# The embedding's gate taken early and corrected expert by expert

## The chip, the cores and the metric

The kernel runs on one core of a Trainium2 chip, in one launch. The metric is the device time of the core in microseconds: 706.93 before, the median of three runs (704.91 to 707.18).

## The reference

One layer of a decoder: token mixers (attention and mLSTM), then a mixture of 32 experts of which each token takes two, then an embedding per layer, and a last norm. The change touches the part from the experts on (T = 256 tokens, D = 1024):

```python
h = h + hierarchical_moe(rmsnorm(h, ffn_norm_g[i]), ...)     # per expert: (silu(x@w_gate) * (x@w_up)) @ w_down, weighted
ple_gate = jax.nn.sigmoid(rmsnorm(h, ple_norm_g[i]) @ w_ple_gate[i])   # 1024 x 1024, float32
h = h + (p[i] @ w_ple_proj[i]) * ple_gate
return rmsnorm(h, final_norm_g)
```

## The kernel before

h is held in SBUF as two blocks b of 128 tokens. The experts e = 0 to 31 are taken in eight quads q of four. For a quad, `dispatch` gathers up to 32 tokens per expert with 0/1 matrices og into xe (matmuls px), and builds the weights dwT (transposes pdw). Then `expert` works on one expert's 32 columns of xe:

- pg, gate and up products: 32 matmuls of 256 columns ("gu" in what follows), each of 32 stationary columns, four side by side on the array; the profile counts two records for a float32 matmul, so 64;
- sg = silu on ScalarE, hid = sg * up on VectorE, pht = its transpose on TensorE, hT = its copy;
- pd, the down products: 16 matmuls (32 records);
- four copies of pd into the expert's 32 rows of eo, ScalarE and VectorE in turn.

After a quad, `combine` spreads eo's 128 rows to the tokens with dwT and adds them to h: four products ps of 512 columns, four adds.

An expert's weights are three loads of 2 MB, two of gu and one of down, all issued by SyncE (SP), each into a slot of the ring `slot` (NRING = 10 slots of 16 KB a partition). A slot that is free goes to the next that asks; a tile that is used to the end keeps it. Up to eight of SP's loads are in flight, since each has one of eight DMA semaphores (DMAHW0 to DMAHW7) to itself.

An expert may have more than 32 tokens. `overflow`, after quad LOOP_AT = 3, counts them and loops over what is left, inside `tc.If(n_rv > 0)`. With these inputs the branch is not taken: the profile has no row of the loop. All engines load n_it and branch there, and instructions do not move across it.

`embed` (p @ w_ple_proj, into pe) stands after quad 5 and uses two slots, wpp and ES; ES stays. The gate comes after the last quad: `load_gate` issues its 4 MB behind expert 31's loads, `split_gate` splits them into two float32r parts (ghi, glo), `transpose_h` does the same for h, and `gate_mm` takes three products for each pair, 120 matmuls. `warm` puts 18 matmuls without use among the last expert's. The tail is tanh, times pe, add to h, square and sum, power on GpSimd (POOL), last scaling, and the output.

A scheduler sets each engine's order when the program is built, after the order of the code and its own costs; on the chip each engine takes its instructions in that order.

Of the kernel before, what the change touches and what calls it, by code (L numbers as in the profile page):

```python
# [36 lines left out]
WARM = (7, 4, 3, 1, 3)  # L37
LO_POOL = (11, 101)
NRING = 10
LOOP_AT = 3  # L40

# [6 lines left out]
def layer(ctx: ExitStack, tc: tile.TileContext, A, dbg=None):  # L48
# [661 lines left out]

    def load_gu(t, e, k0, n):
        nc.sync.dma_start(out=t, in_=wgu_v[e][:, k0:k0 + n])
        return [t[:, k] for k in range(n)]

    def load_expert(e):
        def load_dn(t, j, n):
            nc.sync.dma_start(out=t, in_=wd_v[e][:, j:j + n])
# [67 lines left out]
    def expert(wts, xe, i, eo, row, last=False, rest=None):  # L785


        gu, dn = wts
        pe_ins = []

        def pe(ins):
            if last and pe_ins:
                after(ins, pe_ins[-1])
            pe_ins.append(ins)
            return ins

        def warm(n):
            if last:
                pw = psm.tile([P, 512], F32, name="pw", tag="px", bufs=1)
                for _ in range(n):  # L800
                    pe(mm(pw, identb, identb[:, None, :].to_broadcast([P, 4, P]), start=True, stop=True))

        pg = psm.tile([P, 2, P], F32, name="pg", tag="pg", bufs=2)
        for k in range(KD):
            if k == 4:
                warm(WARM[0])
                if rest is not None:
                    rest(4, ins)
            for j in range(4):
                ins = pe(mm(pg[32 * j:32 * j + 32], xe[:, k, 32 * i:32 * i + 32], gu[k][:, :, j * P:(j + 1) * P],  # L810
                      start=(k == 0), stop=(k == KD - 1)))
        warm(WARM[1])
# [5 lines left out]
        pe(nc.tensor.transpose(pt, hid, ident))  # L818
        warm(WARM[2])
# [3 lines left out]
        for j in range(4):  # L823
            if j == 2:
                warm(WARM[3])
            for c in range(4):
                pe(mm(pd[32 * c:32 * c + 32], hT[:, 32 * j:32 * j + 32], dn[j][:, c * 256:(c + 1) * 256],  # L827
                      start=(j == 0), stop=(j == 3)))
        warm(WARM[4])
        for c in range(4):  # L830
            dst = eo[row:row + 32, c * 256:(c + 1) * 256]
# [13 lines left out]
    def overflow():  # L845
# [32 lines left out]
        with tc.If(n_rv > 0):  # L878
            with tc.For_i(0, n_rv, 1):
# [25 lines left out]
    def embed():  # L905
# [20 lines left out]
        return pe, gfin  # L926


    def load_gate():
# [6 lines left out]
        nc.sync.dma_start(out=gfin, in_=A["final_norm_g"].rearrange("(o d) -> o d", o=1).to_broadcast([P, D]))  # L936
        return out

    def split_gate(k):
        if k % 4 == 0:  # L940
            gw.append((slot([P, 4, D], F32R, name="ghi"), slot([P, 4, D], F32R, name="glo")))
        hi, lo = gw[k // 4]
        return split(hi[:, k % 4], lo[:, k % 4], wpl[k // 4][:, k % 4], lo_on=nc.gpsimd if k in (0, 1, 3, 5) else None)

    for q in range(NQ):
        dwT, xe, rest = dispatch(float(q * QUAD * ESTR) if q else None, code, P)
        eo = mo.tile([P, D], F32, name="eo", bufs=1)
        for i in range(QUAD):
            e = q * QUAD + i
            wt = load_expert(e)  # L950
            if e == NE - 1:
                wpl = load_gate()
            expert(wt, xe, i, eo, 32 * i, last=(e == NE - 1), rest=rest if i == 0 else None)
        if q < NQ - 1:
            for c in range(2):
                for b in range(NB):
                    combine(dwT, eo, P, b, c)
        if q == LOOP_AT:
            overflow()
        if q == NQ - 3:  # L960
            pe, gfin = embed()


    gw = []
    HT = slot([P, 2, KD, T], F32R, name="HT")

    def transpose_h(k):
        pt = psm.tile([P, 2, T], F32, name="pt", tag="tp", bufs=2)
        for b in range(NB):
            for kk in range(2):  # L970
                nc.tensor.transpose(pt[:, kk, b * P:(b + 1) * P], h[:, b, (k + kk) * P:(k + kk + 1) * P], ident)
        for kk in range(2):
            ins = split(HT[:, 0, k + kk], HT[:, 1, k + kk], pt[:, kk], scale=col("g3", k + kk), low=True)
        return ins

    split_gate(0)
    combine(dwT, eo, P, 0, 0)
    combine(dwT, eo, P, 1, 0)
    split_gate(1)
    transpose_h(0)  # L980
    combine(dwT, eo, P, 0, 1)
    lo = transpose_h(2)
    after(combine(dwT, eo, P, 1, 1), lo)
    split_gate(2)
    transpose_h(4)
    transpose_h(6)
    for k in range(3, KD):
        last = split_gate(k)
# [7 lines left out]
    rstd_of(r3[:, 0:NB], ss3[:, 0:NB], D, NB)
    nc.vector.tensor_scalar(r3[:, 0:NB], r3[:, 0:NB], 0.5, None, op0=OP.mult)
    out_v = A["out"].rearrange("o (b p) d -> p (o b) d", p=P)

    parts = [(0, 0, 512, "pg"), (0, 512, 512, "pg"), (1, 0, 512, "ps"), (1, 512, 256, "ps"), (1, 768, 256, "px")]  # L1000
    pg = [psm.tile([P, n], F32, name=f"G{b}{c0}", tag=tag, bufs=1 if tag == "px" else 2) for b, c0, n, tag in parts]

    def gate_mm(i, k):
        b, c0, n, _ = parts[i]
        hi, lo = gw[k // 4]
        bs, cs, kk = slice(b * P, (b + 1) * P), slice(c0, c0 + n), k % 4
        mm(pg[i], HT[:, 0, k, bs], hi[:, kk, cs], start=(k == 0), stop=False)
        mm(pg[i], HT[:, 1, k, bs], hi[:, kk, cs], start=False, stop=False)
        mm(pg[i], HT[:, 0, k, bs], lo[:, kk, cs], start=False, stop=(k == KD - 1))

    hn = []
    junk = mo.tile([P, 512], F32, name="junk", tag="xe", bufs=1)
    for k in range(KD // 2):
        for i in range(len(parts)):
            gate_mm(i, k)
    for i, (b, c0, n, _) in enumerate(parts):
        cs = slice(c0, c0 + n)
        for k in range(KD // 2, KD):
            gate_mm(i, k)
        sg = mo.tile([P, 512], F32, name="sg3", tag="ov")  # L1020
        th = nc.scalar.activation(sg[:, 0:n], pg[i], AF.Tanh, scale=r3[:, b:b + 1])
        nc.vector.scalar_tensor_tensor(sg[:, 0:n], sg[:, 0:n], 1.0, pe[:, b, cs], op0=OP.add, op1=OP.mult)
        hn.append(nc.vector.tensor_tensor(h[:, b, cs], h[:, b, cs], sg[:, 0:n], op=OP.add))
        if i in (0, 2, 3):
            nc.gpsimd.tensor_tensor(y[:, b, cs], h[:, b, cs], gfin[:, cs], op=OP.mult)
        for j in {2: (), 3: (), 4: (2, 3, 4)}.get(i, (i,)):
            pb, p0, m, _ = parts[j]
            s_, rb_ = ss3[:, 2 + j:3 + j], r3[:, 2 + pb:3 + pb]
            sq = nc.scalar.activation(junk[:, 0:m], h[:, pb, p0:p0 + m], AF.Square, scale=D ** -0.5, accum_out=s_)
            after(sq, th)  # L1030
            if j in (1, 3):
                nc.vector.scalar_tensor_tensor(s_, s_, EPS, ss3[:, 1 + j:2 + j], op0=OP.add, op1=OP.add)
            elif j == 4:
                nc.vector.tensor_tensor(s_, s_, ss3[:, 1 + j:2 + j], op=OP.add)
            if j in (1, 4):
                nc.gpsimd.tensor_tensor(rb_, s_, mhalf[:, 0:1], op=OP.pow)
    for b in range(NB):
        for i, (pb, c0, n, _) in enumerate(parts):
            if pb != b:
                continue  # L1040
            cs, rb_ = slice(c0, c0 + n), r3[:, 2 + b:3 + b]
            if i == 0:
                nc.gpsimd.tensor_scalar(y[:, b, cs], y[:, b, cs], rb_, None, op0=OP.mult)
            elif i == 2:
                nc.scalar.activation(y[:, b, cs], y[:, b, cs], AF.Copy, scale=rb_)
            elif i == 3:
                nc.vector.tensor_scalar(y[:, b, cs], y[:, b, cs], rb_, None, op0=OP.mult)
            else:
                after(nc.vector.scalar_tensor_tensor(y[:, b, cs], h[:, b, cs], rb_, gfin[:, cs],
                                                     op0=OP.mult, op1=OP.mult), hn[4])  # L1050
# [46 lines left out]
```

## Time and profile before

| | |
|---|---|
| median of three runs | 706.93 us |
| the profiled run, and its span | 706.04 us, 704.3 us |
| PE (TensorE's matmuls) busy | 560.9 us, 80% |
| DVE (VectorE), ACT (ScalarE), POOL busy | 280.7, 186.1, 38.2 us |
| DMA | 241.98 MB, mean 344 GB/s |
| the chain that ended last | 48% DMA, 44% PE |
| mean granted clock of TensorE | 0.916 of full |

Times in rows are from the span's start. An idle time in brackets is the engine's before the row, with what ended it.

### The profile page before, as it was taken

What the parts mean: (1) busy time and instruction counts of PE and PEld (TensorE: products, weight loads), DVE (VectorE), ACT (ScalarE), POOL (GpSimd) and SP (SyncE); (2) the same over time, 40 slices, a digit from 0 to 9 for tenths busy, and PEclk for the clock granted to TensorE, in tenths of its full rate; (3) what the DMA queues carried; (4) which work ended last, traced back from release to release, by engine and by line L of the source; (5) the groups of instructions that cost most, each with busy time, mean ns of one, the idle gap of its engine ahead of it and who ended that gap; (6) DMA issues with size and microseconds to landing.
All of it is one profiled execution on the core that took longest, in us unless ns stands there. A gap on an engine that the chain in (4) does not pass through costs nothing.

```text
span 704.3 us, 12210 instructions
## 1 busy us (share of the span) xinstructions
PE 560.9 (80%) x5161; PEld 382.3 (54%) x5161; DVE 280.7 (40%) x684; ACT 186.1 (26%) x423; POOL 38.2 (5%) x59
## 2 busy tenths in 40 slices
PE   7999999999999998685686564967746956765894
PEld 7898778899986554342334231733423433432384
DVE  4898667676665343141022024312211310311175
ACT  6675556465453211001000000010000210000163
POOL 3000000001300000000000000000000000000063
PEclk9999999999999999899669886898978997988998
DMA  7946533338777899999999997999999999999921
GB/s 268 429 205 248 228 122 120 120 120 333 305 327 299 333 428 428 428 424 429 423 428 426 430 426 316 429 423 430 426 426 424 425 427 427 429 428 424 419 99 60
DMA packets 22130, 241.98 MB, mean 344 GB/s; under 512 B 4708, under 2 KB 5304, under 8 KB 7096
## 3 DMA queue, kind: packets, MB, share of 16 engines
q1 hardware_dynamic: 22056, 241.16, 82.5%
q8 instruction: 42, 0.69, 0.4%
q14 instruction: 16, 0.13, 0.0%
q10 hardware_dynamic: 16, 0.00, 0.0%
HBM read 240.10 MB, written 1.05 MB: 342 GB/s over the span
## 4 chain that ended last, share of the span: by engine, by line
DMA 48%; PE 44%; DVE 4%; ACT 2%; issue 1%; POOL 1%; POOLq 0%; SPq 0%; DVEq 0%; ACTq 0%
DMA wt<-in_expert_gu 31%; DMA wt<-in_expert_down 17%; PE pg L810 5%; PE po L330 4%; PE po L331 4%; PE po L332 4%; PE ps L839 3%; PE po L347 2%; PE po L346 2%; PE po L348 2%; PE pd L827 2%; PE px L761 2%; PE ps L923 1%; PE pyy L470 1%; DMA wt<-in_w_mix 1%
## 5 line engine op out<-in xcount | busy, mean ns | idle before, releaser
L810 PE MATMUL pg<-wt,xe 128*32 128x256 f32 x2032 | 153.6, 438 | 69.8 <-DMA wt<-in_expert_gu 69.8
L810 PEld LDWEIGHTS pg<-wt,xe 128*32 128x32 f32 x2032 | 73.3, 122 | 136.8 <-issue 55.6
L827 PE MATMUL pd<-wt,hT 128*32 128x256 f32 x1024 | 73.6, 434 | 22.8 <-DMA wt<-in_expert_down 18.6
L833 DVE COPY eo<-pd 32x256 f32<-32x256 f32 x64 | 27.1, 423 | 114.5 <-ACT eo L835 114.4
L827 PEld LDWEIGHTS pd<-wt,hT 128*32 128x32 f32 x1024 | 37.9, 121 | 47.4 <-issue 32.9
L835 ACT ACTIVATE eo<-pd 32x256 f32<-32x256 f32 x64 | 23.9, 374 | 150.3 <-PE pd L827 132.0
L816 DVE TENSOR_TENSOR hid<-sg,pg 128x128 f32<-128x128 f32 x32 | 9.2, 288 | 126.0 <-ACT sg L814 126.0
L220 DVE TENSOR_TENSOR wlo<-wt,whi 128x512 fp32r<-128x512 f32 x76 | 51.5, 685 | 18.3 <-ACT whi L219 18.1
L219 ACT ACTIVATE whi<-wt 128x512 fp32r<-128x512 f32 x77 | 47.3, 626 | 32.0 <-PE po L348 16.7
L814 ACT ACTIVATE sg<-pg 128x128 f32<-128x128 f32 x32 | 8.9, 277 | 168.7 <-PE pg L810 168.6
L761 PE MATMUL px<-og,y 128*128 128x128 f32 x256 | 39.6, 308 | 10.3 <-DVE og L752 6.8
L761 PEld LDWEIGHTS px<-og,y 128*128 128x128 f32 x256 | 35.5, 216 | 22.1 <-PEq L878 7.7
L839 PE MATMUL ps<-eo,dwT 128*128 128x512 f32 x64 | 34.2, 661 | 8.8 <-DVE eo L833 8.7
L332 PE MATMUL po<-XT,wlo 128*128 128x256 f32 x144 | 40.4, 280 | 1.0 <-DVE wlo L220 1.0
L330 PE MATMUL po<-XT,whi 128*128 128x256 f32 x144 | 40.6, 282 | 0.0
L331 PE MATMUL po<-XT,whi 128*128 128x256 f32 x144 | 40.3, 280 | 0.0
L765 DVE TENSOR_TENSOR xe<-px,cols 128x256 f32<-128x256 f32 x32 | 13.6, 424 | 61.5 <-PE pg L810 38.9
L220 POOL TENSOR_TENSOR glo<-wt,ghi 128x1024 fp32r<-128x1024 f32 x4 | 10.6, 2671 | 449.4 <-DMA wt<-in_w_ple_gate 448.6
L332 PEld LDWEIGHTS po<-XT,wlo 128*128 128x128 f32 x144 | 27.0, 188 | 1.2 <-DVE wlo L220 1.2
L220 DVE TENSOR_TENSOR spare<-wt,spare 128x512 fp32r<-128x512 f32 x34 | 23.3, 687 | 9.9 <-ACT spare L219 9.8
L331 PEld LDWEIGHTS po<-XT,whi 128*128 128x128 f32 x144 | 27.1, 188 | 0.2 <-issue 0.2
L330 PEld LDWEIGHTS po<-XT,whi 128*128 128x128 f32 x144 | 27.1, 188 | 0.0
(371 smaller groups left out, 956.9 us busy)
## 6 DMA issues: line engine op xcount, KB each, us to landing
wt<-in_expert_gu SPq DMA_DIRECT2D x63, 2048.0 KB, 38.2
wt<-in_expert_down SPq DMA_DIRECT2D x30, 2048.0 KB, 36.5
wt<-in_w_mix SPq DMA_DIRECT2D x10, 2048.0 KB, 22.2
wt<-in_w_up SPq DMA_DIRECT2D x2, 2048.0 KB, 8.5
wt<-in_w_out SPq DMA_DIRECT2D x2, 2048.0 KB
wt<-in_expert_down SPq DMA_DIRECT2D x4, 1024.0 KB
wt<-in_w_ple_gate SPq DMA_DIRECT2D x4, 1024.0 KB, 27.0
wt<-in_w_mix SPq DMA_DIRECT2D x4, 512.0 KB, 7.0
```

The source lines that it names most:

```text
L219: a = nc.scalar.activation(dst_hi, src, AF.Copy)
L220: b = (lo_on or nc.vector).tensor_tensor(dst_lo, src, dst_hi.bitcast(F32), op=OP.subtract)
L330: mm(out[:, f], whi[:, kk], ahi[:, k], start=(k == 0), stop=False)
L331: mm(out[:, f], whi[:, kk], alo[:, k], start=False, stop=False)
L332: mm(out[:, f], wlo[:, kk], ahi[:, k], start=False, stop=(k == kn - 1))
L346: mm(outs[b], ahi[:, k, bs], whi[:, k - k0], start=(k == 0), stop=False)
L761: ins = mm(px[:, k], y[:, b, kc:kc + P], og[:, b], start=(b == 0), stop=(b == NB - 1))
L810: ins = pe(mm(pg[32 * j:32 * j + 32], xe[:, k, 32 * i:32 * i + 32], gu[k][:, :, j * P:(j + 1) * P], start=(k == 0), stop=(k == KD - 1)))
L827: pe(mm(pd[32 * c:32 * c + 32], hT[:, 32 * j:32 * j + 32], dn[j][:, c * 256:(c + 1) * 256], start=(j == 0), stop=(j == 3)))
L833: nc.vector.tensor_copy(out=dst, in_=pd[32 * c:32 * c + 32])
L835: nc.scalar.activation(dst, pd[32 * c:32 * c + 32], AF.Copy)
L839: mm(ps, dwT[0:n, b], eo[0:n, c * 512:(c + 1) * 512], start=True, stop=True)
```

## The change

The gate is no longer taken at the end. When expert 20's loads are issued (GATE_AT = 5), the gate's weights are loaded into two slots that they keep, and `gate_of_h` takes G = (h * g3) @ w_gate for h as it then is, in plain float32. For each later expert `gate_of_rows` transposes its rows of eo, scales them (eT), multiplies by the gate's weights (pq, the shape of a gu) and keeps the rows in eg_rows; these are spread with dwT and added to G as eo is to h. The root mean square, which multiplies the whole row, comes in at the end. In the last quad the first two experts are combined early, and the last expert's rows go through `gate_of_rows` after the loop. The splits and the warming matmuls go. `embed` moves from quad 5 to behind `overflow`, and takes the load of gfin with it. Experts 16 and 17 are loaded ahead of `overflow`, on GpSimd's queue (NPOOL = 2).

```diff
+GATE_AT = 5
+NPOOL = 2
+    def queue(e):
+        return nc.gpsimd if QUAD * (LOOP_AT + 1) <= e < QUAD * (LOOP_AT + 1) + NPOOL else nc.sync
     def load_gu(t, e, k0, n):
-        nc.sync.dma_start(out=t, in_=wgu_v[e][:, k0:k0 + n])
+        queue(e).dma_start(out=t, in_=wgu_v[e][:, k0:k0 + n])
...
+    def spread(dwT, rows_, r0, r1, b, c):
+        ps = psm.tile([P, 512], F32, name="ps", tag="ps", bufs=2)
+        mm(ps, dwT[r0:r1, b], rows_[r0:r1, c * 512:(c + 1) * 512], start=True, stop=True)
+        return ps
+    def combine(dwT, rows_, r0, r1, b, c, into=None):
+        ps = spread(dwT, rows_, r0, r1, b, c)
+        dst = (h if into is None else into)[:, b, c * 512:(c + 1) * 512]
+        return nc.vector.tensor_tensor(dst, ps, dst, op=OP.add)
...
+    def gate_of_h():
+        GH = slot([P, 4096], name="GH")
...
+        for b in range(NB):
+            for c in range(2):
+                ps = psm.tile([P, 512], F32, name="ps", tag="ps", bufs=2)
+                for k in range(KD):
+                    mm(ps, HT[:, k, b * P:(b + 1) * P], wpg[k][:, c * 512:(c + 1) * 512],
+                       start=(k == 0), stop=(k == KD - 1))
+                nc.scalar.activation(G[:, b, c * 512:(c + 1) * 512], ps, AF.Copy)
+    def gate_of_rows(eo, row, eg):
+        pt = psm.tile([P, KD, CAP], F32, name="pet", tag="tp", bufs=2)
+        rs = slice(row, row + CAP)
+        for k in range(KD):
+            nc.tensor.transpose(pt[:, k], eo[rs, k * P:(k + 1) * P], ident[rs, rs])
+        eT = mo.tile([P, KD, CAP], F32, name="eT", tag="le", bufs=1)
+        nc.vector.tensor_tensor(eT, pt, g3k[:, :, None].to_broadcast([P, KD, CAP]), op=OP.mult)
+        pq = psm.tile([P, 256], F32, name="pq", tag="px", bufs=1)
+        for k in range(KD):
+            for c in range(4):
+                mm(pq[32 * c:32 * c + 32], eT[:, k], wpg[k][:, c * 256:(c + 1) * 256],
+                   start=(k == 0), stop=(k == KD - 1))
+        as_rows(eg, row, pq)
     for q in range(NQ):
...
-            wt = load_expert(e)
-            if e == NE - 1:
-                wpl = load_gate()
-            expert(wt, xe, i, eo, 32 * i, last=(e == NE - 1), rest=rest if i == 0 else None)
+            wt = ahead.pop(e, None) or load_expert(e)
+            if e == QUAD * GATE_AT:
+                wpg = load_gate()
+                G = gate_of_h()
+            expert(wt, xe, i, eo, 32 * i, rest=rest if i == 0 else None)
+            if q >= GATE_AT and e < NE - 1:
+                gate_of_rows(eo, 32 * i, eg_rows)
+            if q == NQ - 1 and i == 1:
+                for into, rows_ in ((None, eo), (G, eg_rows)):
+                    for c in range(2):
+                        for b in range(NB):
+                            combine(dwT, rows_, 0, 64, b, c, into)
...
+            if q >= GATE_AT:
+                for c in range(2):
+                    for b in range(NB):
+                        combine(dwT, eg_rows, 0, P, b, c, G)
         if q == LOOP_AT:
+            for e in range(QUAD * (q + 1), QUAD * (q + 1) + NPOOL):
+                ahead[e] = load_expert(e)
             overflow()
-        if q == NQ - 3:
-            pe, gfin = embed()
+            pe, gfin, eg_rows = embed()
...
+    rows_to_h(0)
+    gate_of_rows(eo, 96, eg_rows)
+    rows_to_h(1)
+    for b in range(NB):
+        for c in range(2):
+            ps = spread(dwT, eg_rows, 64, P, b, c)
+            sg = mo.tile([P, 512], F32, name="sg3", tag="ov")
+            nc.vector.tensor_tensor(sg, ps, G[:, b, cs], op=OP.add)
+            nc.scalar.activation(sg, sg, AF.Tanh, scale=r3[:, b:b + 1])
...
```

SP's order just ahead of the overflow branch, before; gu and down are the loads of experts 14, 15 and 16 (the last two gu):

```order
L712 DMA wt<-in_expert_gu 128x4096 x2
L717 DMA wt<-in_expert_down 128x4096
L712 DMA wt<-in_expert_gu 128x4096 x2
L717 DMA wt<-in_expert_down 128x4096
L712 DMA wt<-in_expert_gu 128x4096 x2
L876 TENSOR_LOAD n_it
L878 COMPARE_AND_BRANCH
```

The same place now:

```order
L717 DMA wt<-in_expert_gu 128x4096 x2
L722 DMA wt<-in_expert_down 128x4096
L717 DMA wt<-in_expert_gu 128x4096 x2
L722 DMA wt<-in_expert_down 128x4096
L899 DMA wpp<-in_w_ple_proj 128x2048
L905 DMA ES<-in_p 128x2x256
L918 DMA ES<-in_final_norm_g 128x1024
L717 DMA wt<-in_expert_gu 128x4096
L868 TENSOR_LOAD n_it
L870 COMPARE_AND_BRANCH
```

Expert 16's gu is gone from SP's queue (it stands with the rest of experts 16 and 17, six loads, in POOL's, ahead of POOL's own load of n_it); the three loads of the embedding, which came after quad 5, stand here, and one gu of expert 18.

SP's order from the end of the branch, in the path that is not taken into the loop, before, with the semaphores that each row waits for (numbers of the tick left out); the first row waits for all of SP's DMAs:

```order
L878 UNCONDITIONAL_BRANCH [waits SP_sequencer_49,DMAHW0_49,DMAHW1_49,DMAHW2_49,DMAHW3_49,DMAHW4_49,DMAHW5_49,DMAHW6_49,DMAHW7_49]
L717 DMA wt<-in_expert_down 128x4096 [waits DMAHW7_49,PE_49]
L712 DMA wt<-in_expert_gu 128x4096 [waits DMAHW0_49,PE_49]
L712 DMA wt<-in_expert_gu 128x4096 [waits DMAHW1_49,PE_49]
L717 DMA wt<-in_expert_down 128x4096 [waits DMAHW2_49,PE_49]
```

And now:

```order
L870 UNCONDITIONAL_BRANCH [waits SP_sequencer_49,DMAHW0_49,DMAHW1_49,DMAHW2_49,DMAHW3_49,DMAHW4_49,DMAHW5_49,DMAHW6_49,DMAHW7_49]
L717 DMA wt<-in_expert_gu 128x4096 [waits DMAHW4_49,DMAHW1_49,PE_49]
L722 DMA wt<-in_expert_down 128x4096 [waits DMAHW5_49,DMAHW2_49,PE_49]
L717 DMA wt<-in_expert_gu 128x4096 [waits DMAHW3_49,DMASW0_49,PE_49]
L717 DMA wt<-in_expert_gu 128x4096 [waits DMAHW4_49,DMASW1_49,PE_49]
L722 DMA wt<-in_expert_down 128x4096 [waits DMAHW5_49,DMASW2_49,PE_49]
```

The wait for all of SP's DMAs stands as it did, and POOL's (DMASW) are not in it. The first two loads behind it are expert 18's second gu and its down; the down's slot is wpp's (DMAHW5), so it waits for the last of the embedding's products, too. Experts 19 and 20, whose slots were those of 16 and 17 (DMASW0 to 5), come behind it.

PE's order in the middle of quad 6, one expert and the next, before:

```order
L810 MATMUL pg<-wt,xe 32x256 x32
L818 MATMUL pht<-ident,hid 128x128
L827 MATMUL pd<-wt,hT 32x256 x16
L810 MATMUL pg<-wt,xe 32x256 x32
L818 MATMUL pht<-ident,hid 128x128
L827 MATMUL pd<-wt,hT 32x256 x16
```

And now, at the same place:

```order
L805 MATMUL pht<-ident,hid 128x128
L811 MATMUL pd<-wt,hT 32x256 x16
L959 MATMUL pet<-ident,eo 128x32 x8
L965 MATMUL pq<-wt,eT 32x256 x32
L798 MATMUL pg<-wt,xe 32x256 x32
L805 MATMUL pht<-ident,hid 128x128
L811 MATMUL pd<-wt,hT 32x256 x16
```

Between the down products of one expert and the gu of the next stand the eight transposes of eo's rows and the 32 gate products.

## Rows read from the trace of the kernel before

**Rows 1.** The page, its span and the GB/s of 40 equal slices
```profile
span 704.3 us, 12210 instructions
...
GB/s 268 429 205 248 228 122 120 120 120 333 305 327 299 333 428 428 428 424 429 423 428 426 430 426 316 429 423 430 426 426 424 425 427 427 429 428 424 419 99 60
```

**Rows 2.** The page, the chain that ended last, by engine and by line
```profile
DMA 48%; PE 44%; DVE 4%; ACT 2%; issue 1%; POOL 1%; POOLq 0%; SPq 0%; DVEq 0%; ACTq 0%
...
DMA wt<-in_expert_gu 31%; DMA wt<-in_expert_down 17%; PE pg L810 5%; PE po L330 4%; PE po L331 4%; PE po L332 4%; PE ps L839 3%; PE po L347 2%; PE po L346 2%; PE po L348 2%; PE pd L827 2%; PE px L761 2%; PE ps L923 1%; PE pyy L470 1%; DMA wt<-in_w_mix 1%
```

**Rows 3.** Timeline (start, us, engine, line, [idle before]): PE's waits for gu
```profile
415.51 3.30 PE L810 MATMUL pg<-wt,xe 128*32 128x256 f32 x32 [1.88 <-DMA wt<-in_expert_gu]
...
479.07 3.00 PE L810 MATMUL pg<-wt,xe 128*32 128x256 f32 x32 [2.87 <-DMA wt<-in_expert_gu]
...
537.81 3.59 PE L810 MATMUL pg<-wt,xe 128*32 128x256 f32 x32 [2.87 <-DMA wt<-in_expert_gu]
...
660.09 1.93 PE L810 MATMUL pg<-wt,xe 128*32 128x256 f32 x32 [1.27 <-DMA wt<-in_expert_gu]
```

**Rows 4.** Timeline: SP's issues and PE at the overflow branch
```profile
386.15 5.23 SPq L712 DMA_DIRECT2D wt<-in_expert_gu  x2
...
430.34 0.34 SPq L717 DMA_DIRECT2D wt<-in_expert_down  x1
...
439.58 5.68 PE L761 MATMUL px<-og,y 128*128 128x128 f32 x25 [6.81 <-DVE og L752]
```

**Rows 5.** Stretches (busy by engine, clock, DMA share, GB/s): the dry spot
```profile
430.00:431.00 1.00, 1.00 (x3) 0.35 (x2) 0.69 (x1) 0.00 (x0) 0.00 (x0) 0.50 0.00 0
```

**Rows 6.** Timeline: PE's products of the embedding
```profile
549.87 0.60 PE L917 MATMUL pp<-ident,ES 128*128 128x128 f32 x4
...
551.16 7.13 PE L923 MATMUL ps<-wpp,ES 128*128 128x512 f32 x16 [0.69 <-ACT ES L918]
```

**Rows 7.** Timeline: PE's durations by kind
```profile
546.08 3.96 PE L839 MATMUL ps<-eo,dwT 128*128 128x512 f32 x8 [0.94 <-DVE eo L833]
...
558.13 2.01 PE L761 MATMUL px<-og,y 128*128 128x128 f32 x16
...
566.51 1.93 PE L827 MATMUL pd<-wt,hT 128*32 128x256 f32 x32 [0.38 <-DVE hT L821]
...
568.26 1.91 PE L810 MATMUL pg<-wt,xe 128*32 128x256 f32 x32
...
670.18 0.82 PE L971 MATMUL pt<-ident,h 128*128 128x128 f32 x6
```

**Rows 8.** Stretches: the first quad, which waits for no weights
```profile
225.35:261.65 36.30, 35.53 (x456) 20.93 (x457) 13.65 (x40) 5.76 (x14) 0.00 (x0) 1.00 0.89 363
```

**Rows 9.** Timeline: waits inside one expert
```profile
571.96 1.93 PE L810 MATMUL pg<-wt,xe 128*32 128x256 f32 x32 [1.79 <-DMA wt<-in_expert_gu]
...
574.62 0.33 PE L818 MATMUL pht<-ident,hid 128*128 128x128 f32 x1 [0.72 <-DVE hid L816]
...
574.98 0.29 DVE L821 COPY hT<-pht 128x128 f32<-128x128 f32 x1 [0.42 <-PE pht L818]
...
576.96 1.93 PE L827 MATMUL pd<-wt,hT 128*32 128x256 f32 x32 [2.01 <-DMA wt<-in_expert_down]
...
578.95 0.37 ACT L835 ACTIVATE eo<-pd 32x256 f32<-32x256 f32 x1 [4.71 <-PE pd L827]
...
580.21 0.43 DVE L833 COPY eo<-pd 32x256 f32<-32x256 f32 x1 [0.44 <-ACT eo L835]
```

**Rows 10.** Timeline: the end
```profile
665.11 1.07 PE L827 MATMUL pd<-wt,hT 128*32 128x256 f32 x16
...
686.88 0.69 ACT L1021 ACTIVATE sg<-G,r 128x512 f32<-128x512 f32 x1 [4.75 <-PE G L1009]
...
687.60 0.69 DVE L1022 SCALAR_TENSOR_TENSOR sg<-sg,ES 128x512 f32<-128x512 f32 x1 [3.47 <-ACT sg L1021]
...
700.02 0.48 DVE L1049 SCALAR_TENSOR_TENSOR y<-h,r,ES 128x256 f32<-128x256 f32 x1
```

More of the change, by code (lines that the diff above doesn't have):

```diff
@@ L36 @@
 NWARM = 27
-WARM = (7, 4, 3, 1, 3)
 LO_POOL = (11, 101)
@@ L716, in load_dn @@
         def load_dn(t, j, n):
-            nc.sync.dma_start(out=t, in_=wd_v[e][:, j:j + n])
+            queue(e).dma_start(out=t, in_=wd_v[e][:, j:j + n])
             return [t[:, i] for i in range(n)]
@@ L783, in dispatch, with expert @@
         return dwT, xe, gather if off is None else None
-    def expert(wts, xe, i, eo, row, last=False, rest=None):
+    def expert(wts, xe, i, eo, row, rest=None):
         gu, dn = wts
[L789 to L801, printed above, removed]
         pg = psm.tile([P, 2, P], F32, name="pg", tag="pg", bufs=2)
         for k in range(KD):
[L805 to L808, printed above, removed]
+            if k == 4 and rest is not None:
+                rest(4, ins)
             for j in range(4):
-                ins = pe(mm(pg[32 * j:32 * j + 32], xe[:, k, 32 * i:32 * i + 32], gu[k][:, :, j * P:(j + 1) * P],
-                      start=(k == 0), stop=(k == KD - 1)))
-        warm(WARM[1])
+                ins = mm(pg[32 * j:32 * j + 32], xe[:, k, 32 * i:32 * i + 32], gu[k][:, :, j * P:(j + 1) * P],
+                         start=(k == 0), stop=(k == KD - 1))
         sg = mo.tile([P, P], F32, name="sg")
@@ L817, in expert @@
         pt = psm.tile([P, P], F32, name="pht", tag="tp", bufs=2)
-        pe(nc.tensor.transpose(pt, hid, ident))
-        warm(WARM[2])
+        nc.tensor.transpose(pt, hid, ident)
         hT = mo.tile([P, P], F32, name="hT")
@@ L823, in expert, with as_rows @@
         for j in range(4):
-            if j == 2:
-                warm(WARM[3])
             for c in range(4):
-                pe(mm(pd[32 * c:32 * c + 32], hT[:, 32 * j:32 * j + 32], dn[j][:, c * 256:(c + 1) * 256],
-                      start=(j == 0), stop=(j == 3)))
-        warm(WARM[4])
+                mm(pd[32 * c:32 * c + 32], hT[:, 32 * j:32 * j + 32], dn[j][:, c * 256:(c + 1) * 256],
+                   start=(j == 0), stop=(j == 3))
+        as_rows(eo, row, pd)
+    def as_rows(rows_, row, pd):
         for c in range(4):
-            dst = eo[row:row + 32, c * 256:(c + 1) * 256]
+            dst = rows_[row:row + 32, c * 256:(c + 1) * 256]
             if c % 2:
@@ L925, in embed @@
                 nc.scalar.activation(pe[:, b, c * 512:(c + 1) * 512], ps, AF.Copy, scale=0.5)
-        return pe, gfin
+        nc.sync.dma_start(out=gfin, in_=A["final_norm_g"].rearrange("(o d) -> o d", o=1).to_broadcast([P, D]))
+        return pe, gfin, ES[:, 0:1024]
     def load_gate():
@@ L935, in load_gate @@
             out.append(wt)
[L936 to L943, printed above, removed]
+        return [wt[:, k] for wt in out for k in range(4)]
@@ L945, in layer @@
+    ahead = {}
     for q in range(NQ):
@@ L964, in layer @@
[L964 to L976, printed above, removed]
@@ L996, in layer @@
[L996 to L1009, printed above, removed]
@@ L1011, in layer @@
[L1011 to L1042, printed above, removed]
-                nc.gpsimd.tensor_scalar(y[:, b, cs], y[:, b, cs], rb_, None, op0=OP.mult)
[L1044 to L1050, printed above, removed]
+    out_v = A["out"].rearrange("o (b p) d -> p (o b) d", p=P)
@@ new lines, in layer @@
+    for b in range(NB):
+        for c in range(2):
+            cs, i = slice(c * 512, (c + 1) * 512), 2 * b + c
+            ps = spread(dwT, eg_rows, 64, P, b, c)
+            sg = mo.tile([P, 512], F32, name="sg3", tag="ov")
+            nc.vector.tensor_tensor(sg, ps, G[:, b, cs], op=OP.add)
+            nc.scalar.activation(sg, sg, AF.Tanh, scale=r3[:, b:b + 1])
+            nc.vector.scalar_tensor_tensor(sg, sg, 1.0, pe[:, b, cs], op0=OP.add, op1=OP.mult)
+            nc.vector.tensor_tensor(h[:, b, cs], h[:, b, cs], sg, op=OP.add)
+            nc.scalar.activation(junk, h[:, b, cs], AF.Square, scale=D ** -0.5, accum_out=ss3[:, 2 + i:3 + i])
+            if i != 3:
+                nc.gpsimd.tensor_tensor(y[:, b, cs], h[:, b, cs], gfin[:, cs], op=OP.mult)
+        s_, rb_ = ss3[:, 2 + 2 * b:3 + 2 * b], r3[:, 2 + b:3 + b]
+        nc.vector.scalar_tensor_tensor(s_, s_, EPS, ss3[:, 3 + 2 * b:4 + 2 * b], op0=OP.add, op1=OP.add)
+        nc.gpsimd.tensor_tensor(rb_, s_, mhalf[:, 0:1], op=OP.pow)
+        for c in range(2):
+            cs = slice(c * 512, (c + 1) * 512)
+            if b == 1 and c == 1:
+                nc.vector.scalar_tensor_tensor(y[:, b, cs], h[:, b, cs], rb_, gfin[:, cs], op0=OP.mult, op1=OP.mult)
+            elif c == 0:
+                nc.scalar.activation(y[:, b, cs], y[:, b, cs], AF.Copy, scale=rb_)
+            else:
+                nc.gpsimd.tensor_scalar(y[:, b, cs], y[:, b, cs], rb_, None, op0=OP.mult)
```

39 lines of the change are left out of this document (19 added, 20 removed).

## The prediction

> **What bounds the kernel now.** I read the page first. Over its 40 slices the GB/s row stands at 423 to 430 from slice 15 almost to the end, with one dent to 316 [rows 1]; the chain that ended last is 48% DMA, and its two largest members are the loads of expert weights [rows 2]. So the expert loop runs at the pace of the weight stream. Next the timeline, for the moments at which PE waits for a landing: the second half of expert 19's gate and up weights (gu) is there at 479.07, expert 23's at 537.81, expert 31's at 660.09, expert 15's at 415.51 [rows 3]. From 19 to 23 lie 12 loads of 2 MB in 58.74 us, 4.90 each, 14.7 an expert. From 23 to 31 lie 24 loads (117.5) and 4.8 more: the embedding's wpp and p. From 15 to 19 lie 12 loads and 4.8 more: the stream ran dry. Why shows in the issues: SP issues expert 16's gu at 386.15 and nothing more until 430.34, since it stands at the overflow branch, and there, by the order, it waits until all its own DMAs have landed [rows 4]; in 430 to 431 nothing moves [rows 5]. The last down product begins at 665.11 and takes 1.07 us [rows 10]; from 666.2 to the span's end at 704.3 lie 38.1 us in which the gate is worked out while its weights land.
>
> So the change can win at two places, the tail and the dry spot, and PE, which waits for weights in most experts, has to carry new work.
>
> **Part by part.** Times are against the profiled span; the run took 706.04, 1.7 more than its span, and lies 0.1% under the median of 706.93.
>
> The tail. It loses the splits, 120 matmuls of gate and the 18 warming matmuls. What is left after the last down product: four copies into eo, over 1.8 us after it [rows 9]; eight transposes and four products into h in between (0.14 and 0.99 each [rows 7]), to 5.7; the 32 matmuls of the last expert's gate rows, which have the shape of a gu, two times 1.75 [rows 7], to 9.3; two of its copies and the first product, to 11.3. Then four parts with three DVE passes of 0.69 each [rows 10], 8.3 us, and about 1.1 for waits on ACT's tanh of 0.69, to 20.7. A square, its sum and the power, and a last pass, about 2.8 more; from the start of the last pass to the span's end the row of before shows 4.3, of which 0.5 is the pass [rows 10], so 3.8. Sum 27.3, against 38.1: 10.8 less. But the 4 MB of gate weights, which landed beside that tail, and gfin are now ahead of the last expert in the stream: two loads' worth, 9.8, and 0.5 MB, 1.2. Together 11.0. Tail and stream cancel out.
>
> The stream up to the gate. Expert 20's last load landed at 479.07 + 4 x 4.90 = 498.7. Without a dry spot it is 4.8 earlier; wpp, p and gfin go ahead of it, 6.0; the gate behind it, 9.8. The gate's weights land at 509.7 + H, where H is what runs dry in the new kernel.
>
> H, the six loads on GpSimd's queue. They go out as slots come free, the first when expert 12's down weights are used (about 378.5), while nine loads are still queued on SP. No row shows two queues with large loads at once. The bounds: if SP's queue goes first, expert 15 lands as before at 420.4, SP passes the branch as before, and six loads cover the wait: H = 0. If they share, loads of experts 16 and 17 land ahead of expert 15's, whose last one comes as late as 420.4 + 6 x 4.90 = 449.8. PE then leaves the branch 19.2 later (420.4 to 439.58 in [rows 4]), at 469.0, and has the embedding first, since that stands behind the branch now: 8.4 at full clock (549.87 to 558.29 [rows 6]), up to twice that at half; right behind the branch px ran at 0.23 us a record (25 in 5.68 [rows 4]) against 0.13 (16 in 2.01 [rows 7]), so I take 12, to 481. Only then is wpp's slot free, for which expert 18's down load stands at the head of SP's queue with all others behind it. SP itself was held until expert 18's first load, the last it had issued, landed near 461. The stream is dry from the second load of 18 (about 471) on. A restart cost 9.6 from issue to first landing (430.34 to 479.07 - 8 x 4.90), so that load lands at 490.6 instead of 470.5: H = 20. I take the shared case: both queues hold the same kind of 2 MB load, and nothing in the rows ranks them. Both ends stay in the range. The Trainium skill, "DMA: Bandwidth & Descriptors", section "Queues, rings and completion order", says that an engine takes turns between the queue rows it has work for, a packet at a time; no row here shows it. By that rule H is 20 and the time the forecast below, by a queue that waits its turn it would be 20 less.
>
> PE from the gate's landing to the end of the last down product. The gate of h is 32 products of 512 columns; 16 records (eight such products) took 7.13 [rows 6], 0.89 each. Four run while the second half of the weights lands, 28 are left: 24.9. Then 12 down products of 1.75, 11 gu of 3.5 (two times 1.75), 11 gate rows of 3.5 (same shape), 88 transposes of 0.14, 12 transposes of hid of 0.33, two dispatches of two px groups of 2.0 with four 0.33 transposes, and 24 products into h or G of 0.99 [rows 7]: 21.0 + 38.5 + 38.5 + 12.3 + 4.0 + 9.3 + 23.8 = 147.4. Bare sum 172.3. The stream has 33 loads in that stretch, 161.7, and with the last down product 162.8. So PE is behind the stream by 10 before it has waited for anything, and it waits: in the new order of experts 25 to 27 nothing or little stands between gu and hid's transpose, or between that and the down product. Such a place costs 0.7 from the end of gu (573.9 to 574.62) and again about 0.65 [rows 9]; the gate rows' transposes wait for the copies of eo, 1.8, then for eT. The one stretch of before that ran without waiting for weights, the first quad, took 36.30 us at granted clock 1.00 [rows 8], where the same prices give 33.0 (four gu 14.0, four down 7.0, px 6.0, products 4.0, transposes 2.0): a tenth more. A tenth on 172.3 gives 189.5; walking quads 5 to 7 row by row with the waits above gives 194. I take 191. The bounds are 163 (everything hidden) and 205.
>
> Does the ring hide it? Of ten slots ES, GH and the two gate tiles keep four to the end; six are left, two experts. While PE is in the gate of h, five loads land (24.5 us) and then the stream stops for want of a slot, and from there PE sets the pace.
>
> Costed at nothing: DVE's and ACT's additions per expert (one eT pass, four copies of 0.4, two of them on each) lie beside PE's 10 us; the embedding before quad 4 is in H where it counts, and elsewhere hidden, because PE waits for weights in quad 4; without that cover it costs 8.4 and gives back as much after quad 5.
>
> Sum: 509.7 + 20 + 191 + 27.3 + 1.7 = 749.7, so 750 us.
>
> **The rivals.**
> 1. SP's queue goes first (or gets most of the turns): H = 0, the rest as above: 730. For it: SP's loads were queued first. Against it: nothing ranks the two. With a quarter of the engines' time for GpSimd's queue H would be about 4, so this case reaches to 734.
> 2. Faster: PE hides the gate. If the three last quads fit into the stream's gaps, the stretch is 162.8 instead of 191 and with H = 0 the end is 509.7 + 162.8 + 27.3 + 1.7 = 701.5; the 4.8 of the dry spot is the whole gain. It decides from PE work under 163 us in that stretch. For it: PE waits 1.3 to 2.9 us for weights again and again in before [rows 3]. Against it: the bare sum of 172.
> 3. PE hides the gate, but the dry spot is there: 701.5 + 20 = 721.5.
> 4. The change doesn't do what it says: GpSimd's loads do not move until SP's have drained, and the dry spot stays at 4.8: 735.
>
> **How the numbers follow.** The forecast (shared queues, PE sets the pace) 0.50; rival 1 0.29; rival 2 0.08; rival 3 0.09; rival 4 0.04. The forecast's own range, from PE's 180 to 205 and the embedding's 8 to 17, is 735 to 766. The range that holds the time 8 times in 10 reaches down through rivals 1, 3 and 4 to 712 and leaves out rival 2; up it ends at 764. A change of under 0.3% (705 to 709) is what a measurement of this kernel cannot tell from none. Faster than that takes rival 2: 0.07; within it, rival 2 with a few us of PE left over: 0.04; slower 0.89.
>
> **What would show it.** In the new profile: GB/s at 428 in slices up to the overflow branch, then a gap of over 10 us at about 470 to 482, with SP's next down load issued when the embedding's products end. For rival 1: no gap, and expert 15 used near 420. At the gate of h: 32 products back to back, some 28 us, with the stream stopping near their end, and from there a GB/s row under 428 while PE stays over 90% busy at clock 1.00, and a chain that is PE and not DMA; the quads from 24 on some 60 us long. The tail after the last down product 27 us. The forecast is wrong if PE still waits for weight landings in quads 6 and 7, if the stretch from the gate's landing to the last down product is under 175, or if the tail is not over 8 us shorter.

## The result and the profile after

The changed kernel takes 755.31 us (median of four runs, 748.96 to 756.24) beside 706.57 for the kernel before: 1.068 times, with an interval of 1.0625 to 1.0733. The profiled execution is the fastest of the four, 748.96, with a span of 747.3; the accounts below are made against it, and a second profile, among the experiments, is of an execution that took 753.13.

The page of the changed kernel, its busy line and its GB/s row:

```profile
span 747.3 us, 13919 instructions
...
PE 621.4 (83%) x5991; PEld 403.4 (54%) x5991; DVE 300.3 (40%) x727; ACT 189.6 (25%) x437; POOL 31.6 (4%) x62
...
GB/s 275 428 147 326 124 114 113 128 221 337 409 248 293 429 428 425 428 426 427 425 427 426 431 423 306 203 428 425 426 305 427 424 322 430 425 314 428 179 2 56
...
PE 32%; DVE 3%; ACT 1%; issue 1%; POOL 1%; POOLq 0%; ACTq 0%; DVEq 0%
PE pg L798 8%; PE pq L965 6%; PE ps L827 4%; PE pd L811 4%; PE ps L947 4%; PE px L766 2%; PE pet L959 1%; PE ps L915 1%; ACT eo L822 1%; DVE eo L820 1%; PE pht L805 1%; DVE hid L803 0%; ACT sg L801 0%; DVE hT L807 0%; PE pdw L785 0%
```

Against [rows 1] and [rows 2]: the stream, level at 427 before, has a dent at 306 and 203 and four more later (305, 322, 314, then 179), and the chain is another one. Its shares add up to only 38%, since it is followed back no further than 464.45, to PE's first product behind the branch; in that part no DMA is left in it, and of the time ahead of the branch it says nothing. The new work stands in it: the gate rows (pq), the gate of h (L947).

What happens at the branch shows on PE, in the timeline of its waits (start, us, engine, line, [idle before]):

```profile
388.55 3.64 PE L798 MATMUL pg<-wt,xe 128*32 128x256 f32 x32 [5.32 <-DMA wt<-in_expert_gu]
...
398.44 3.64 PE L811 MATMUL pd<-wt,hT 128*32 128x256 f32 x32 [5.05 <-DMA wt<-in_expert_down]
...
408.69 3.64 PE L798 MATMUL pg<-wt,xe 128*32 128x256 f32 x32 [6.61 <-DMA wt<-in_expert_gu]
418.39 3.26 PE L798 MATMUL pg<-wt,xe 128*32 128x256 f32 x32 [6.06 <-DMA wt<-in_expert_gu]
...
451.25 3.64 PE L811 MATMUL pd<-wt,hT 128*32 128x256 f32 x32 [0.38 <-DVE cnt L843]
...
464.45 0.63 PE L909 MATMUL pp<-ident,ES 128*128 128x128 f32 x4 [3.39 <-PEq L870]
...
465.80 8.65 PE L915 MATMUL ps<-wpp,ES 128*128 128x512 f32 x16
```

SP's loads land 9.7 to 10.3 us apart, about twice the 4.90 of before: GpSimd's six loads, issued from 379.49 to 421.99, take every second turn. Expert 15's down product begins at 451.25 instead of 420.49, and PE leaves the branch at 464.45. SP's issues in the changed kernel, and the stretch in which nothing moves:

```profile
449.63 11.54 SPq L717 DMA_DIRECT2D wt<-in_expert_gu  x2
474.48 0.33 SPq L722 DMA_DIRECT2D wt<-in_expert_down  x1
...
515.48 2.79 SPq L717 DMA_DIRECT2D wt<-in_expert_gu  x2
549.82 0.33 SPq L722 DMA_DIRECT2D wt<-in_expert_down  x1
```
```profile
468.00:474.00 6.00, 6.00 (x14) 2.57 (x13) 0.00 (x0) 1.79 (x3) 0.00 (x0) 0.92 0.00 0
```

The gap in the stream is there, though about 7 us long (from 467.8 to 475.2) where over 10 were forecast, and expert 18's down load goes out as the embedding's products end. But PE is busy through all of it, and from here to the end it waits for no weights. Its quad 4, the gate of h, and the next experts' down products:

```profile
483.87 1.93 PE L811 MATMUL pd<-wt,hT 128*32 128x256 f32 x32
...
489.85 1.93 PE L811 MATMUL pd<-wt,hT 128*32 128x256 f32 x32
...
503.12 1.93 PE L811 MATMUL pd<-wt,hT 128*32 128x256 f32 x32
...
518.73 1.12 PE L947 MATMUL ps<-wt,GH 128*128 128x512 f32 x2 [0.84 <-ACT GH L941]
...
520.56 26.77 PE L947 MATMUL ps<-wt,GH 128*128 128x512 f32 x62
...
547.83 1.93 PE L811 MATMUL pd<-wt,hT 128*32 128x256 f32 x32
...
559.86 1.93 PE L811 MATMUL pd<-wt,hT 128*32 128x256 f32 x32
```

Experts 16 to 19, whose weights all land before PE wants them, take 6 to 7 us each; the gate of h takes 27 us in one piece; with its gate rows an expert then takes 10 to 13.5 us within a quad. SP issues nothing from 518.27 to 549.82: the ring is full. The stretch from the fourth gate product (three of 0.86 after 520.56, so 523.2) to the end of the last down product (717.65 + 1.93), by engine, with PE's waits from 547 on in the second fence:

```profile
523.20:719.58 196.38, 178.34 (x2065) 91.80 (x2063) 53.23 (x124) 22.69 (x61) 0.00 (x0) 1.00 0.84 350
```
```profile
PE pht L805 <- DVE hid L803: 7.5, 10, 1.1
PE pd L811 <- DVE hT L807: 3.5, 9, 0.4
PE pet L959 <- ACT eo L822: 3.0, 6, 0.5
PE pq L965 <- DVE eT L961: 2.1, 4, 0.5
```

PE is 91% busy at full clock, the DMA engines 84%, and each wait is for VectorE or ScalarE inside an expert.

### The profile page after: what moved, and what is told of

Same layout as the page of the kernel before. It is cut to its first block, busy times and chain, and to the rows that moved or that the text cites. A ratio compares the mean times of both kernels' runs of the same rounds, so it can differ in the third digit from the quotient of the medians.

```text
span 747.3 us, 13919 instructions
## 1 busy us (share of the span) xinstructions
PE 621.4 (83%) x5991; PEld 403.4 (54%) x5991; DVE 300.3 (40%) x727; ACT 189.6 (25%) x437; POOL 31.6 (4%) x62
## 5 line engine op out<-in xcount | busy, mean ns | idle before, releaser
L798 PE MATMUL pg<-wt,xe 128*32 128x256 f32 x2032 | 147.2, 409 | 49.7 <-DMA wt<-in_expert_gu 49.7
L798 PEld LDWEIGHTS pg<-wt,xe 128*32 128x32 f32 x2032 | 67.8, 115 | 103.7 <-issue 35.6
L965 PE MATMUL pq<-wt,eT 128*32 128x256 f32 x768 | 44.2, 380 | 2.1 <-DVE eT L961 2.1
L827 PE MATMUL ps<-eo,dwT 128*128 128x512 f32 (+1 forms) x72 | 36.4, 620 | 5.3 <-DVE eo L820 5.0
L766 PEld LDWEIGHTS px<-og,y 128*128 128x128 f32 x256 | 31.7, 196 | 12.4 <-issue 4.8
L766 PE MATMUL px<-og,y 128*128 128x128 f32 x256 | 35.0, 287 | 2.2 <-DVE xe L770 1.9
L965 PEld LDWEIGHTS pq<-wt,eT 128*32 128x32 f32 x768 | 24.8, 110 | 20.4 <-DVE eT L961 3.4
L833 DVE TENSOR_TENSOR h<-ps,h 128x512 f32<-128x512 f32 x36 | 24.9, 692 | 11.2 <-PE ps L827 11.1
L947 PE MATMUL ps<-wt,GH 128*128 128x512 f32 x64 | 27.9, 594 | 0.8 <-ACT GH L941 0.8
L820 DVE COPY ES<-pq 32x256 f32<-32x256 f32 x24 | 10.1, 423 | 45.3 <-ACT ES L822 45.1
```

What stands on the lines that cost most here:

```text
L766: ins = mm(px[:, k], y[:, b, kc:kc + P], og[:, b], start=(b == 0), stop=(b == NB - 1))
L798: ins = mm(pg[32 * j:32 * j + 32], xe[:, k, 32 * i:32 * i + 32], gu[k][:, :, j * P:(j + 1) * P], start=(k == 0), stop=(k == KD - 1))
L820: nc.vector.tensor_copy(out=dst, in_=pd[32 * c:32 * c + 32])
L827: mm(ps, dwT[r0:r1, b], rows_[r0:r1, c * 512:(c + 1) * 512], start=True, stop=True)
L947: mm(ps, HT[:, k, b * P:(b + 1) * P], wpg[k][:, c * 512:(c + 1) * 512], start=(k == 0), stop=(k == KD - 1))
L965: mm(pq[32 * c:32 * c + 32], eT[:, k], wpg[k][:, c * 256:(c + 1) * 256], start=(k == 0), stop=(k == KD - 1))
```

## The experiments

Names that begin with b_ are edits of the kernel before, those with a_ of the changed one. Each verdict is against runs of the kernel before on the same chip (706.5 to 707.0). Where a run is set beside the changed kernel, it is beside that kernel's median of 755.31; a second median of it, in after_again, is 753.12, so such a difference is good to some 2 us.

**b_queue2: the queue alone.**

```diff
+    def queue(e):
+        return nc.gpsimd if 16 <= e < 18 else nc.sync
...
         if q == LOOP_AT:
+            for e in (16, 17):
+                ahead[e] = load_expert(e)
             overflow()
```

> The kernel before with one part of the change alone: the loads of experts 16 and 17 go ahead of the overflow branch on GpSimd's queue; the embedding, the gate and the tail stay as they were. Theory (PE's work after the gate's landing makes the loss, the queue little): nearly no change, 701 to 709, because the two queues share and both run out near the same time, so the dry spot of 4.8 us is hidden only in part. Rival Q (the moved loads and the dry spot behind them cost most of the 49 us): 720 or more.

712.33 us (eight runs, 708.04 to 715.16), ratio 1.0079 [1.0054, 1.0105]: 5.9 slower. The theory's range is missed by 3, the rival's by 8. GpSimd's loads do not cover the branch; they make it later. In the trace of this kernel SP's issues are

```profile
381.34 0.33 SPq L721 DMA_DIRECT2D wt<-in_expert_down  x1
432.23 9.67 SPq L716 DMA_DIRECT2D wt<-in_expert_gu  x2
460.28 0.34 SPq L721 DMA_DIRECT2D wt<-in_expert_down  x1
```

SP still issues expert 18's two gu ahead of the branch, as slots come free, then waits until they have landed. They are the last in flight (GpSimd's last went out at 422.63), so the stream runs dry behind them as it did before, and PE comes out of the branch at 467.62 instead of 439.58. The stream-bound quads behind give most of that back, since the ring is full by then.

**b_queue3: three experts on the queue.** The same with `16 <= e < 19`.

> As the kernel before with experts 16, 17 and 18 (nine loads) on GpSimd's queue ahead of the overflow branch. Theory: the last of the nine are issued after SP's own loads have landed, so the stream has work across the branch, and the dry spot of 4.8 us goes: 700 to 704. Rival Q: slower than the kernel before, 720 or more.

715.33 us, ratio 1.0129 [1.0113, 1.0145]. The theory was wrong on this kernel, and the rival's 720 is not reached either. Its page:

```profile
GB/s 266 430 195 281 191 119 119 119 124 385 297 278 290 398 430 427 425 427 428 425 427 428 426 428 427 417 109 426 427 428 422 426 428 426 426 426 429 420 111 60
```

The hole (109, a slice of 17.8 us) is deeper than the 316 of before. With expert 15 late, the ring is full of weights for experts 16 to 18, and no load can go out until PE has used some. More loads ahead make that worse.

**b_gated2: the same two experts, issued later.** GpSimd waits for expert 15's second gu tile.

```diff
+        if gate is not None:     # expert 16; gate = one column of expert 15's second gu tile
+            nc.gpsimd.tensor_copy(out=t0[:, 0, 0, 0:1], in_=gate)
```

> The kernel before with experts 16 and 17 on GpSimd's queue as in b_queue2, but held back: GpSimd first copies one column of expert 15's second gu tile into expert 16's slot, so that its six loads go out only when expert 15's gu have landed (near 415) and SP has one to three loads left. Theory (the moved loads cost because they share the engines with expert 15's and land too early, and so run out with SP's): with three of them still in flight when SP's queue is dry, the dry spot of 4.8 us goes: 700 to 705. Rival (the branch itself, or the queue's own cost, makes the 6 us of b_queue2, whenever the loads go out): 710 or more.

703.72 us, ratio 0.9953 [0.9939, 0.9966]: 3.1 faster than the kernel before, and faster than both. In its timeline GpSimd's six issues begin at 417.34, where they began at 379.11 in b_queue2:

```profile
416.65 0.19 POOL L726 COPY wt<-wt 128x1 f32<-128x1 f32 x1 [195.78 <-DMA wt<-in_expert_gu]
417.34 1.32 POOL L716 DMA_DIRECT2D wt<-in_expert_gu  x2 [0.50 <-issue]
```
```profile
GB/s 268 430 208 243 216 141 121 120 121 306 318 344 296 298 428 428 426 427 428 427 426 427 425 429 426 428 426 424 428 427 424 427 426 428 425 428 428 416 68 61
```

The GB/s row has no dent left. So it is the moment of the moved loads that costs, not their queue.

**b_hold3: fewer slots.**

```diff
+            if e == 20:
+                held = [slot([P, 4096]) for _ in range(3)]    # kept until expert 29
```

> The kernel before with three of the ten ring slots held (one memset each, read once after expert 29) from expert 20 on, so that with ES six are left in quads 6 and 7, as in the changed kernel. Theory: two experts' worth of slots keeps the stream going as long as PE is faster than the stream, so 704 to 711. Rival S (it is the lack of slots that stops the stream in the changed kernel): tens of us, 725 or more.

706.41 us, ratio 1.0002 [0.9993, 1.0011]. Six slots are enough as long as PE is faster than the stream; rival S falls.

**a_sp_only: the queue's part in the changed kernel.** `NPOOL = 0`.

> The changed kernel with NPOOL = 0: experts 16 and 17 are loaded on SP's queue behind the branch again, all else as changed. Theory: the queue part alone cost the kernel before 5.9 us, and gives back about as much here: 745 to 752. Rival Q (together with the embedding behind the branch the moved loads cost far more than alone): under 740. A second rival (PE sets the end, so a drier stream costs nothing): 754 to 757.

739.03 us, ratio 1.0453 [1.0426, 1.0479]: 16.3 less than the changed kernel, nearly three times the 5.9 that the theory took from b_queue2; it lies 1 under rival Q's bound, so rival Q holds, narrowly. The timeline of this kernel:

```profile
432.72 0.63 PE L909 MATMUL pp<-ident,ES 128*128 128x128 f32 x4 [3.13 <-PEq L870]
...
488.60 1.93 PE L811 MATMUL pd<-wt,hT 128*32 128x256 f32 x32 [1.24 <-DMA wt<-in_expert_down]
...
505.77 1.37 PE L947 MATMUL ps<-wt,GH 128*128 128x512 f32 x2 [2.42 <-DMA wt<-in_w_ple_gate]
```

PE leaves the branch 31.7 us earlier than in the changed kernel, then waits for the stream in quad 4, and reaches the gate of h 13.0 earlier, where it waits for the gate's weights. 32 us late at the branch cost 13 at the gate: the rest is what the full ring gives back.

**a_gated2: that part, gated.** The edit of b_gated2 on the changed kernel.

> The changed kernel with its six loads on GpSimd's queue held back as in b_gated2. Theory (their cost is that PE leaves the branch late; PE's work after the gate is the rest): the 16 us that a_sp_only gave back come back here too, and since the stream does not run dry now, perhaps some more of its 4.8: 733 to 740. Rival (with the embedding behind the branch the moved loads cost whatever their moment): 748 or more.

735.8 us, ratio 1.0407 [1.039, 1.0425], 19.5 less than the changed kernel. The theory holds: with the embedding behind the branch as well, the moment of the loads decides.

**a_embed4: the dry spot's cause.**

```diff
+        if q == LOOP_AT + 1:
+            pe, gfin, eg_rows = embed()
         if q == LOOP_AT:
             ...
-            pe, gfin, eg_rows = embed()
```

> The changed kernel with the embedding behind quad 4 instead of behind the branch. It asks what the moved loads cost there (16 us by a_sp_only). Theory E (the stream runs dry since expert 18's down load waits for the slot of the embedding's weights): that wait is gone, and 6 to 13 us come back: 742 to 749. Rival P (PE comes late out of the branch, by 32 us, and has its own work to do from there to the end, the embedding in either place): 752 to 757.

755.78 us, ratio 1.0705 [1.0685, 1.0726]: no change. Theory E falls, P holds. In the stretch that was empty the stream now runs (a shorter lull, 55 GB/s, stands at 474 to 477), and nothing is won: the second fence is PE at the gate of h, four products of which are done at 527.2, no earlier than in the changed kernel.

```profile
468.00:474.00 6.00, 6.00 (x47) 5.52 (x46) 2.11 (x7) 0.00 (x0) 0.00 (x0) 0.68 0.67 284
```
```profile
524.59 26.77 PE L947 MATMUL ps<-wt,GH 128*128 128x512 f32 x62
```

**a_no_rows: without the rows of experts 20 to 29.**

```diff
-            if q >= GATE_AT and e < NE - 1:
+            if e == NE - 2:
                 gate_of_rows(eo, 32 * i, eg_rows)
```

> The changed kernel without the gate rows of experts 20 to 29 and without the sums into G (those of 30 and 31 and the last product stay; the output leaves those experts' part out of the gate). The gate of h stays where it is. Theory (PE's whole work against the stream): PE loses 34 us of gate rows, 10 of their transposes, 12 of products and their waits, falls under the stream's 163, and catches up the 27 us of the gate of h, which the six slots cover: 709 to 722. Rival L (the lump of 27 us in the gate of h is the loss, since the stream stops behind it; the rows lie in the gaps between landings): 740 or more.

726.02 us, ratio 1.0294 [1.026, 1.0328]: 29.3 less, 4 above the theory's range, 14 below the rival's. PE waits for the stream again: its waits of this kernel from 547 on,

```profile
PE pg L798 <- DMA wt<-in_expert_gu: 19.0, 9, 3.0
PE pd L811 <- DMA wt<-in_expert_down: 6.8, 4, 2.1
```

where the changed kernel has none.

**a_no_h: without the gate of h.** Its transposes and products are replaced by `nc.scalar.activation(G[:, b], h[:, b], AF.Copy)`.

> The changed kernel without the transposes and the 32 products of the gate of h (G is a copy of h by ScalarE instead, so the output is another one). Theory: PE's stretch falls from 199 to about 170, still a little over the stream's 163: 722 to 732. Rival L (the lump is the whole loss): 704 to 714.

738.21 us, ratio 1.0446 [1.0397, 1.0495]: 17.1 less, where the theory had about 27 and the rival 41 or more: the theory's range is missed by 6. Expert 20's down product comes 30.5 us earlier than in the changed kernel (517.37 for 547.83), but the next ones come 20, 15 and 14 us apart, where the changed kernel has 12, 10 and 12:

```profile
517.37 1.93 PE L811 MATMUL pd<-wt,hT 128*32 128x256 f32 x32 [0.39 <-DVE hT L807]
...
521.93 5.35 PE L953 MATMUL pq<-wt,eT 128*32 128x256 f32 x64 [0.52 <-DVE eT L949]
...
532.33 3.57 PE L798 MATMUL pg<-wt,xe 128*32 128x256 f32 x32 [2.96 <-DMA wt<-in_expert_gu]
...
537.34 1.93 PE L811 MATMUL pd<-wt,hT 128*32 128x256 f32 x32 [0.38 <-DVE hT L807]
...
552.21 1.93 PE L811 MATMUL pd<-wt,hT 128*32 128x256 f32 x32 [0.38 <-DVE hT L807]
...
566.67 3.46 PE L811 MATMUL pd<-wt,hT 128*32 128x256 f32 x32 [1.67 <-DMA wt<-in_expert_down]
```

PE waits 4.8 us for weights in this stretch, and two experts' gate rows take 5.35 each, at a granted clock of 0.67, where the changed kernel's take 3.64. So part of the lump was covered; that in it the stream fills the ring and quad 5 lives on that fits these waits, but they alone do not make up the difference.

**a_gate7: fewer rows, the gate later.** `GATE_AT = 7`.

> The changed kernel with GATE_AT = 7: the gate of h is taken behind seven quads, and only the four experts of the last quad add rows to it. PE loses some 45 us of rows, transposes and products. Theory: the loss is PE's excess over the stream from the gate's landing on, and that landing moves to 637; behind it stand 25 us of the gate of h and 58 us of four experts, against 44 us of stream, so the excess of some 36 us stays: 743 to 757. Rival R (each expert's rows are what costs, wherever they stand): 712 to 724.

743.01 us, ratio 1.0508 [1.0484, 1.0533], at the lower edge of the theory's range; rival R, 712 to 724, falls. Eight experts without gate rows save 12 us of the 45 that PE does less. The gate of h begins at 640.21, and then four experts are left in which nothing can be caught up.

**after_again: the changed kernel once more.**

> The changed kernel once more, unchanged: the profiled execution took 748.96, the timed ones 754.7 to 756.2. If the difference is TensorE's clock, a profile near 755 shows the same waits and a lower granted clock in some stretch; if it is the loads' order, other moments of landing between 380 and 480.

753.12 us (747.47 to 753.42). The profiled execution took 753.13, so the 755 of the timed ones is not explained by it. PE's waits behind the branch are the same; PE leaves the branch at 467.92 instead of 464.45, and this is most of the 4.1 us between the two spans. Ahead of it, in the timelines of the first and of the second profile:

```profile
457.10 3.96 PE L827 MATMUL ps<-eo,dwT 128*128 128x512 f32 x8 [2.21 <-DVE eo L820]
```
```profile
456.52 5.46 PE L827 MATMUL ps<-eo,dwT 128*128 128x512 f32 x8 [3.92 <-DVE eo L820]
...
467.92 1.09 PE L909 MATMUL pp<-ident,ES 128*128 128x128 f32 x4 [5.94 <-PEq L870]
```

In both PE had waited for weights for 70 us. The products ps then ran at a granted clock of 1.00 in the first and 0.71 in the second, which is 1.5 us. The larger part, 2.6 us, is PE's idle time at the branch (3.39 and 5.94, ended by its own sequencer), and no row gives a reason for it.

## Why the prediction was right, and where it was not

The forecast, 750.0, lies 0.7% under the median of 755.31. By its own steps, against the profiled execution and the one of after_again:

| step | forecast | profiled | second profile |
|---|---|---|---|
| expert 15's last load has landed, its down product begins | 449.8 | 451.25 | 450.67 |
| PE leaves the branch | 469.0 | 464.45 | 467.92 |
| the embedding's products end | 481 | 474.45 | 478.63 |
| four products of the gate done (509.7 + H) | 529.7 | 523.2 | 527.3 |
| from there to the last down product's end | 191 | 196.4 | 196.4 |
| the tail (to the span's end) | 27.3 | 27.7 | 27.7 |
| around the span | 1.7 | 1.7 | 1.7 |
| sum | 749.7 | 749.0 | 753.1 |

**The tail** was right: 27.7 against 38.1 in [rows 10]. That the 4.5 MB now ahead of expert 31 cost as much in the stream cannot be seen here, where PE sets the pace. a_sp_only bears it out roughly: there PE waits for the gate's weights, and its fourth product is done at 511.3, where 509.7 and the 4.8 of the old dry spot make 514.5, so the loads ahead cost some 3 us less than forecast.

**The shared queues** were right in kind. SP's loads land 9.7 to 10.3 us apart while GpSimd's are in flight. This agrees with the Trainium skill ("DMA: Bandwidth & Descriptors", "Queues, rings and completion order"), by which an engine takes turns between the queue rows. Rivals 1 and 4 fall with it.

**H is the step that failed**, in its size and in part of its reason. 523.2 - 509.7 makes H 13.5 where 20 was written; in the second profile it is 17.6. The landing that H stands for came about as the forecast had it: PE left the branch 4.5 earlier than forecast and had done the embedding 6.5 earlier, so expert 18's down load went out sooner, and the last of the gate's loads, issued at 494.81, lands 28.7 later, at 523.5 instead of 529.7:

```profile
wt<-in_w_ple_gate SPq DMA_DIRECT2D x1, 1024.0 KB, 28.7
```

But the gap in the stream is not what makes this time, and that part of the reason fails. In a_embed4 the same load is issued at 493.87 and lands 25.5 later, at 519.4, and PE's four products are done at 527.2, no earlier. PE comes to the gate of h by its own pace, about as the weights land, and does not wait for them. It leaves the branch 25 us later than in [rows 4] and then has work of its own in every stretch: the embedding 10, quad 4 at 6 us an expert, the transposes of h. What the moved loads really cost is the difference to a_sp_only: 16.3 us in the medians.

**PE's stretch** was right as the bound and 5 too short. PE waited 18.0 us in it (196.4 - 178.3), against 18.7 in the forecast (191 - 172.3); its work was 178.3 where the bare sum had 172.3. Which kind carries the 6 cannot be read from the lines, since the scheduler lays the rows of one kind between those of another and their spans overlap. The walk through the quads, 194, was nearer than the value taken. This error (5.4) and that of H (6.5) have opposite signs and nearly cancel in the profiled execution, which is luck: the sum was better than its terms. In the second profile H is only 2.4 too long, and the sum of the steps lies 3 over the forecast. The forecast's own range ends at 766, where its terms (PE's 205, the embedding's 17) give 769; the time lies under both.

**Rivals 2 and 3** (PE hides the gate) fall: PE has not one wait for weights after the branch. a_no_rows and a_no_h show that it is the total that counts. Either piece of the gate's work alone costs less than its own length (17.1 of some 30; 29.3 of the 56 and their waits), and in both PE waits for weights again. That the stream fills the ring while PE is held up and PE catches up behind, and that with both pieces there is nothing to catch up with, is the reading that fits; how much of each difference it makes was not separated. The 48.7 us to the kernel before are then 16.3 of the moved loads and 32.3 (739.03 against 706.73) of all else. Most of that is PE's work beyond the stream: in a_sp_only the stretch from the fourth gate product to the last down product's end takes 198.1 (511.3 to 709.44) without a wait for weights, 35 more than the stream's 162.8, where the forecast had 28 (191 - 162.8). The shorter tail and the loads moved ahead make the rest.

One thing was overlooked: the forecast took the move of the loads and its dry spot as one price. b_gated2 shows that the move itself can be worth 3.1 us, if the loads start when SP's queue is nearly empty.

## What to carry to other kernels

In a loop that a weight stream bounds, add up the compute engine's whole work from the point where the new work starts and set it against the stream's time for the same stretch: single pieces hide in the ring in part, their sum does not, and the 10 us that a shorter tail gave here are little beside an excess of 35. In this kernel a second queue did not put its loads behind those already queued: SP's landed at half their pace beside it, so loads that are meant to cover a drain had to start when the first queue was nearly empty. A small copy on the issuing engine, which waits for a landing, did that: the same loads cost 5.9 us when they went out early and gained 3.1 when they were tied to a landing. And a term for a stretch without traffic belongs in the sum only if somebody waits there.

## What the runs showed of the hardware

- Two queues with 2 MB loads each shared the engines evenly: landings on SP's queue came 9.7 to 10.3 us apart instead of 4.90, with 423 to 431 GB/s in all, as with one queue alone.
- In the stretch of waits at 420 to 450, where PE works 12.71 of 30 us in one profile of the changed kernel and 12.93 in the other, the granted clock was 0.67 and 0.57, between the two levels of 1.2 and 2.4 GHz. In the first 5 us behind the branch it was 0.66 and 0.50 (the lower level), in the next 5 us 1.00 (the upper) and 0.96.
- The changed kernel scattered more than the one before, 747.5 to 756.2 over its eight runs against 704.9 to 707.8. Long waits alone do not show as the cause: in b_queue3 PE works 11.04 us of the same 30, at a clock of 0.66, and its four runs lie within 714.6 to 716.0.
